# Expert stage of a two-layer trunk: PSUM banks of the gather, scatter and one-hot steps taken in turn from two pools

## The chip, the cores and the metric

The kernel runs on one core of a Trainium2 chip. The metric is the device time of one execution in microseconds (us). Most executions of one kernel agree within 0.3%. The engines are named as the profile names them: PE (TensorE, matmuls; PEld are its weight loads), DVE (VectorE), ACT (ScalarE), POOL (GpSimd) and SP (SyncE, which issues the transfers).

## The reference

A post-norm trunk of two layers on 256 tokens of width 1024. Each layer has a mixing sublayer (three groups of heads) and a channel sublayer: a dense SwiGLU in layer 0, and in layer 1 eight SwiGLU experts of inner width 3584, of which each token uses two:

```python
logits = (xt @ w_router).astype(jnp.float32)
top_v, top_i = lax.top_k(logits, TOP_K)                 # TOP_K = 2 of N_EXPERTS = 8
top_w = jax.nn.softmax(top_v, axis=-1)
gates = jnp.sum(jax.nn.one_hot(top_i, N_EXPERTS) * top_w[..., None], axis=1)
for e in range(N_EXPERTS):
    y = y + gates[:, e:e+1] * ((jax.nn.silu(xt @ w_gate[e]) * (xt @ w_up[e])) @ w_down[e])
x = layer_norm(DN_ALPHA * x + y, ln2_g[l], ln2_b[l])
```

## The kernel before

All weights are float32 and come from memory once. A weight chunk of 128x2048 (`raw`) is split into a rounded high part on ACT (`whi`, line 151) and the rest on DVE (`wlo`, line 152), and a product of such numbers is three matmuls: high by high, low by high, high by low (`mm3`, lines 161 to 163). For the expert stage only the tokens that chose an expert are used. Experts are handled in pairs (pr = e // 2).

The expert stage is `moe`. It goes over 8 experts e and 7 pieces m of the inner width (512 each). I call one pair (e, m) a pass. A pass has three blocks of matmuls: gate (G, tile `eg`), up (U, tile `eg`), and the down product of the pass before (D, tiles `y`, two banks that are held for all 7 passes of an expert). Each block needs two split chunks, one for each half of the block, so that a pass has six splits on ACT and six on DVE. Between G and U stands the transpose of the pass before (`ht`, line 166), which is copied out by ACT and DVE (`wk`, lines 943 and 945).

An expert with at most 64 tokens takes a light form at run time (lines 897, 898 and 971: two matmuls instead of three); otherwise the heavy form runs (lines 161 to 163). Both stand in the program, behind a branch (line 856) that reads a register. In this run experts 0, 3, 5 and 6 are heavy, and 1, 2, 4 and 7 light.

Between the blocks the kernel does small steps, one at each `point()`. A list `chores` holds them, and three points lie in each pass (behind G, behind U, behind D):

- gather (`gx`, line 741): one-hot matrices `pm` pick the tokens of the next pair of experts. Eight steps, one for each quarter of the width, high part (`xth`) and low part (`xtl`); four matmuls each. A high step is copied out by ACT (line 751, two copies), a low step by DVE (line 749, two copies). This happens in passes m = 2 to 4 of experts 1, 3 and 5.
- one-hot step (`gsb`, lines 800 and 802): the transposed one-hot matrix and the gate weights of one expert, copied out by ACT (lines 805, 806). Two steps in each of experts 0, 2, 4 and 6.
- scatter (`sc`, lines 993 and 994): adds an expert's result to the tokens. Four steps in passes m = 1 and 2 of the expert that follows, each added to `r` (the residual) by one DVE instruction (line 999).

PSUM is used through two pools of four tiles of 128x512 float32 each: `acc` and `wps`. In the expert stage `wps` holds the `eg` tiles, two for each pass, and `acc` holds the two `y` tiles and, in the two banks that are left, `ht` and the steps:

```python
acc = ctx.enter_context(tc.tile_pool(name="acc", bufs=4, space=PS))
wps = ctx.enter_context(tc.tile_pool(name="wps", bufs=4, space=PS))
def bank(pool, name):
    return pool.tile([P, 512], F32, tag="acc" if pool is acc else "wps", name=name)
```

The copies out of PSUM are held back by `defer(n, ...)` until n more half-splits (1024 wide) are recorded. The framework's scheduler gives each tile a bank when one is free, and puts every engine's instructions in an order by that; an instruction that writes a bank waits for the last reader of the tile that had it before. So which bank a step gets decides both the order on the engines and the waits. Blocks behind a branch stay whole.

Of the kernel before, what the change touches and what calls it, by code (L numbers as in the profile page):

```python
# [86 lines left out]
def trunk(ctx: ExitStack, tc: tile.TileContext, x, consts, mconsts, vecs, lnrows, w_in, w_uq, w_ukv, w_o,  # L87
# [6 lines left out]
# [5 lines that stand above are left out]
# [38 lines left out]
    last = [None, None]  # L137
# [17 lines left out]
    def hold_splits(*steps):  # L155
        plan.clear()
        for ins, eng, n in steps:
            plan.extend([(ins, eng)] * n)
# [18 lines left out]
    def ln_sum(r, src, ps, s, scale=ALPHA, halves=(0, 1)):  # L177
        for n in halves:
            cs = slice(n * 512, (n + 1) * 512)
            nc.vector.scalar_tensor_tensor(r[:, cs], src[:, cs], scale, ps[n], ALU.mult, ALU.add, accum_out=s[:, n:n + 1])  # L180
            ln_half(r, n, s)
# [455 lines left out]
    def moe(pool, raws2, raws3, r, gb, rw):  # L637
# [87 lines left out]
        def gather(pr):  # L725
            pm = pool.tile([P, 2, 256], F32R, tag="pm", name="pm")
            for tt in range(2):
                for j in range(2):
                    ip = nc.vector.tensor_scalar(pm[:, tt, j * P:(j + 1) * P], iota, posm[:, tt, 2 * pr + j:2 * pr + j + 1],
                                            None, ALU.is_equal)  # L730
            if pr == 0:
                hold_splits(((), None, 2), ((pw,), nc.gpsimd, 2), ((i1, pw), nc.gpsimd, 1), ((i1, ip), None, 3))
            xgs = [pool.tile([P, KD, P, 2], F32R, tag="xg", name="xg", bufs=3) for j in range(2)]

            def half_part(k2, hl, n=0):
                src = (xth, xtl)[hl]
                b = bank(acc, "gx")
                for kk in range(2):
                    k = 2 * k2 + kk
                    for tt in range(2):  # L740
                        nc.tensor.matmul(b[:, kk * 256:(kk + 1) * 256], src[:, tt, k * P:(k + 1) * P], pm[:, tt, :],
                                         start=(kk == 0 and tt == 0), stop=(kk == 1 and tt == 1))

                def copies():
                    bv = b.rearrange("p (a b) -> p a b", b=256)
                    for j in range(2):
                        o = xgs[j][:, 2 * k2:2 * k2 + 2, :, hl]
                        if hl:
                            nc.vector.tensor_copy(o, bv[:, :, j * P:(j + 1) * P])
                        else:  # L750
                            nc.scalar.copy(o, bv[:, :, j * P:(j + 1) * P])

                defer(n, copies)

            def part(k2):
                for hl in range(2):
                    half_part(k2, hl)

            return pm, xgs, part, half_part
# [26 lines left out]
        def gather2(pr, pm):  # L786
            gs = pool.tile([P, 2], F32, tag="gs", name="gs")
            pT = pool.tile([P, 2, 2, P], F32R, tag="pTm", name="pTm")
            sc[pr] = [(gs[:, j:j + 1], pT[:, j]) for j in range(2)]

            for j in range(2):
                for tt in range(2):
                    nc.vector.tensor_scalar(pm[:, tt, j * P + 64:(j + 1) * P], iota[:, 64:P],
                                            posds[0][:, tt, 2 * pr + j:2 * pr + j + 1], None, ALU.is_equal)
            pmf = pm.bitcast(F32)

            def one(j):
                b = bank(acc, "gsb")
                for tt in range(2):
                    nc.tensor.matmul(b[:, 256:264], pmf[:, tt, j * P:(j + 1) * P], gates[:, tt, :], start=(tt == 0), stop=False)  # L800
                for tt in range(2):
                    nc.tensor.matmul(b[:, tt * P:(tt + 1) * P], pmf[:, tt, j * P:(j + 1) * P], ident, start=False, stop=(tt == 1))

                def copies():
                    nc.scalar.copy(gs[:, j:j + 1], b[:, 256 + 2 * pr + j:257 + 2 * pr + j])
                    nc.scalar.copy(pT[:, j, :, :], b[:, 0:256].rearrange("p (a b) -> p a b", b=P))

                defer(CHORE_N, copies)

            return one  # L810
# [3 lines left out]
        def defer(n, fn):  # L814
            if n:
                later.append([n, fn])
            else:
                fn()


        chores = []
        points = [0]

        def point():
            points[0] += 1
            if chores and chores[0][0] <= points[0]:
                chores.pop(0)[1]()
# [161 lines left out]
            nc.vector.scalar_tensor_tensor(y[1], yb[n], gs, y[0].bitcast(F32), ALU.mult, ALU.subtract)  # L989

        def scatter(n, tt, y, pT, last=False):
            b = bank(acc, "sc")
            nc.tensor.matmul(b, pT[:, tt, :], y[0], start=True, stop=False)
            nc.tensor.matmul(b, pT[:, tt, :], y[1], start=False, stop=True)
            if last:
                ln_sum(ya[tt], ya[tt], {n: b}, fsums[tt], 1.0, (n,))
            else:
                cs = slice(n * 512, (n + 1) * 512)
                defer(CHORE_N, lambda: nc.vector.tensor_tensor(ya[tt][:, cs], ya[tt][:, cs], b, ALU.add))
# [80 lines left out]
        sc = {}  # L1080
# [5 lines left out]
        def finish(e, m, ht, fold_up=None, fe=None, hook=None):  # L1086
            if m == 0:
                yb[e] = [bank(acc, "y") for _ in range(2)]
            down(e, m, ht, yb[e], fold_up, fe, hook)
            if m == FM - 1:  # L1090
                gs, pT = sc[e // 2][e % 2]
                if e == NE - 1:
                    ys = [[wk[:, 1024 * n + 512 * i:1024 * n + 512 * i + 512] for i in range(2)] for n in range(2)]
                    for n in range(2):
                        scaled(n, yb[e], gs, ys[n])
                    for n in range(2):
                        for tt in range(2):
                            scatter(n, tt, ys[n], pT, True)
                else:
                    yt = pool.tile([P, 2, 2, 512], F32R, tag="xg", name="ys", bufs=3)  # L1100
                    ys = [[yt[:, n, i] for i in range(2)] for n in range(2)]

                    def both():
                        for n in range(2):
                            scaled(n, yb[e], gs, ys[n])

                    defer(4, both)
                    for n in range(2):
                        for tt in range(2):
                            chores.append((points[0] + 3, lambda n=n, tt=tt: scatter(n, tt, ys[n], pT)))  # L1110
# [19 lines left out]
        for e in range(NE):  # L1130
            pr = e // 2
# [163 lines left out]
    with tc.tile_pool(name="spl2", bufs=3, reuse_waits="tile") as spl[0], \  # L1295
            tc.tile_pool(name="moe", bufs=1, reuse_waits="tile") as mp, tc.tile_pool(name="raws3", bufs=ORDER.count(2), reuse_waits="tile") as raws3, \
            tc.tile_pool(name="raws2", bufs=ORDER.count(1), reuse_waits="tile") as raws2:
        xo = moe(mp, raws2, raws3, r, gb, rw)
        for tt in range(2):
            for n in range(2):  # L1300
                cs = slice(n * 512, (n + 1) * 512)
                nc.sync.dma_start(out[0, tt * P:(tt + 1) * P, cs], xo[tt][:, cs])
# [108 lines left out]
```

## Time and profile before

| what | value |
|---|---|
| median of 3 runs | 1471.09 us (1469.09 to 1473.74) |
| the profiled execution | 1468.16 us, span 1466.0 us |
| PE busy | 1359.3 us, 93% of the span |
| DVE busy | 1176.5 us, 80% |
| ACT busy | 997.0 us, 68% |
| mean granted TensorE clock | 0.987 of full speed |

The expert stage runs from about 485 us to 1450 us. Busy shares are means over passes of two kinds, so the table of stretches in the rows below is read pass by pass: a heavy pass without steps takes 17.1 us and a light one 14.4 us. A stretch there goes from one `ht` to the next, so it holds U and D of one pass and G of the next. Its columns are: from:to and the length in us, then the busy time (and instructions) of PE, PEld, DVE, ACT and POOL, the granted TensorE clock (1.00 is full speed), the share of time in which the 16 DMA engines were busy, and GB/s. The profiled execution lies 2.93 us under the median of the runs.

### The profile page before, as it was taken

The numbers are of one execution on the slowest core, as the hardware profiler recorded it, in microseconds if no ns is written. First come the engines' busy times: TensorE is split into PE (matmuls) and PEld (weight loads), VectorE is DVE, ScalarE is ACT, GpSimd is POOL, SyncE is SP. The second block draws the span as 40 slices with busy tenths as digits, with TensorE's granted clock in tenths as the row PEclk, the third lists the DMA queues.
The fourth block names the chain that finished last, engine by engine and source line by source line (L and its number), as shares of the span: only waits on it lengthen the run. The fifth ranks groups of instructions, "written<-read, shape, count | busy, mean of one in ns | idle before, by whom it ended". The sixth has DMA issues, their size and how long they took to land. (4 is left out here: it accounts for less than half of the span.)

```text
span 1466.0 us, 18597 instructions
## 1 busy us (share of the span) xinstructions
PE 1359.3 (93%) x6927; PEld 1118.0 (76%) x6927; DVE 1176.5 (80%) x1256; ACT 997.0 (68%) x1073; POOL 78.4 (5%) x113
## 2 busy tenths in 40 slices
PE   7999999999999899988989999998999999999895
PEld 6987999998987688766666677866677787787663
DVE  6577655557677788899999987898998788788996
ACT  3564444444565677788978877787986777778794
POOL 3011000004102100000000000000000000000101
PEclk9999999999999999999999999999999999999998
DMA  6733555544534699999999998899998799899980
GB/s 264 276 135 115 189 186 186 188 157 153 194 116 201 231 339 356 375 365 349 420 406 369 419 382 323 325 367 348 407 419 342 295 357 357 311 358 389 357 363 30
DMA packets 63513, 429.46 MB, mean 293 GB/s; under 512 B 7058, under 2 KB 7570, under 8 KB 15268
## 3 DMA queue, kind: packets, MB, share of 16 engines
q1 hardware_dynamic: 63364, 427.81, 76.4%
q8 instruction: 81, 1.33, 0.4%
q14 instruction: 36, 0.29, 0.1%
q0 software_dynamic: 32, 0.03, 0.0%
HBM read 426.76 MB, written 1.05 MB: 292 GB/s over the span
## 5 line engine op out<-in xcount | busy, mean ns | idle before, releaser
L152 DVE TENSOR_TENSOR wlo<-raw,whi 128x2048 fp32r<-128x2048 f32 (+4 forms) x475 | 911.0, 1939 | 158.3 <-ACT whi L151 156.7
L151 ACT CAST whi<-raw 128x2048 fp32r<-128x2048 f32 (+4 forms) x482 | 771.0, 1619 | 250.5 <-PE gu L585 44.0
L898 PE MATMUL eg<-wlo,xg 128*128 128x512 f32 x448 | 185.6, 414 | 22.1 <-DVE wlo L152 19.0
L162 PE MATMUL eg<-wlo,xg 128*128 128x512 f32 x448 | 178.0, 397 | 0.8 <-DVE wlo L152 0.3
L161 PE MATMUL eg<-whi,xg 128*128 128x512 f32 x448 | 178.6, 399 | 0.0
L897 PE MATMUL eg<-whi,xg 128*128 128x512 f32 x448 | 178.4, 398 | 0.0
L163 PE MATMUL eg<-whi,xg 128*128 128x512 f32 x448 | 176.6, 394 | 0.0
L898 PEld LDWEIGHTS eg<-wlo,xg 128*128 128x128 f32 x448 | 84.4, 188 | 70.4 <-DVE wlo L152 54.9
L971 PE MATMUL y<-wlo,wk 128*128 128x512 f32 x224 | 94.2, 421 | 17.0 <-DVE wlo L152 15.8
L162 PEld LDWEIGHTS eg<-wlo,xg 128*128 128x128 f32 x448 | 86.9, 194 | 21.5 <-DVE wlo L152 5.4
L163 PEld LDWEIGHTS eg<-whi,xg 128*128 128x128 f32 x448 | 86.7, 194 | 17.3
L584 PE MATMUL gu<-xhi,whi 128*128 128x256 f32 x352 | 99.8, 283 | 0.1
L585 PE MATMUL gu<-xlo,whi 128*128 128x256 f32 x352 | 99.7, 283 | 0.2 <-DVE xlo L224 0.2
L161 PEld LDWEIGHTS eg<-whi,xg 128*128 128x128 f32 x448 | 86.9, 194 | 16.7
L586 PE MATMUL gu<-xhi,wlo 128*128 128x256 f32 x352 | 99.6, 283 | 0.0
L897 PEld LDWEIGHTS eg<-whi,xg 128*128 128x128 f32 x448 | 84.9, 189 | 15.0 <-ACT whi L151 0.5
L971 PE MATMUL y<-whi,wk 128*128 128x512 f32 x224 | 90.3, 403 | 3.6 <-DVE wk L945 1.5
L162 PE MATMUL y<-wlo,wk 128*128 128x512 f32 x224 | 88.0, 393 | 3.6 <-DVE wlo L152 3.4
L161 PE MATMUL y<-whi,wk 128*128 128x512 f32 x224 | 87.5, 392 | 0.4 <-ACT hh L919 0.4
L163 PE MATMUL y<-whi,wk 128*128 128x512 f32 x224 | 87.3, 390 | 0.0
L971 PEld LDWEIGHTS y<-wlo,wk 128*128 128x128 f32 x224 | 44.1, 197 | 42.7 <-DVE wlo L152 36.0
L584 PEld LDWEIGHTS gu<-xhi,whi 128*128 128x128 f32 x352 | 67.6, 192 | 0.7 <-DVE xlo L224 0.3
(313 smaller groups left out, 2111.8 us busy)
## 6 DMA issues: line engine op xcount, KB each, us to landing
raw<-in_e_gate SPq DMA_DIRECT2D x112, 1024.0 KB, 7.1
raw<-in_e_up SPq DMA_DIRECT2D x110, 1024.0 KB, 7.2
raw<-in_e_down SPq DMA_DIRECT2D x108, 1024.0 KB, 7.4
raw<-in_ffn_gu SPq DMA_DIRECT2D x22, 1024.0 KB, 4.8
raw<-in_ffn_dn SPq DMA_DIRECT2D x11, 1024.0 KB, 4.7
raw<-in_w_in SPq DMA_DIRECT2D x10, 960.0 KB, 4.7
raw<-in_w_o SPq DMA_DIRECT2D x8, 1024.0 KB, 6.7
gb<-in_lnrows SPq DMA_DIRECT2D x8, 512.0 KB, 5.3
```

The lines of the kernel that those rows point to most:

```text
L151: last[0] = nc.scalar.copy(hi[:, :n], src)
L152: last[1] = (eng or nc.vector).tensor_tensor(lo[:, :n], src, hi.bitcast(F32)[:, :n], ALU.subtract)
L161: nc.tensor.matmul(o, ahi, bhi, start=start, stop=False)
L162: nc.tensor.matmul(o, ahi, blo, start=False, stop=False)
L163: return nc.tensor.matmul(o, alo, bhi, start=False, stop=stop)
L584: nc.tensor.matmul(o, hi[:, cs], xhi[:, k, :], start=(g == 0 and k == 0), stop=False)
L585: nc.tensor.matmul(o, hi[:, cs], xlo[:, k, :], start=False, stop=False)
L586: nc.tensor.matmul(o, lo[:, cs], xhi[:, k, :], start=False, stop=(g == 1 and k == 7))
L897: nc.tensor.matmul(bs[g], x2, sp[k // 4][0][:, cs], start=(k == 0), stop=False)
L898: nc.tensor.matmul(bs[g], x2, sp[k // 4][1][:, cs], start=False, stop=(k == 7))
L971: nc.tensor.matmul(yb[n], h2, sp[j // 2][i][:, j % 2 * D + n * 512:j % 2 * D + n * 512 + 512], start=(m == 0 and j == 0 and i == 0), stop= ...
```

## The change

A counter gives the steps their pool: odd ones take a bank of `wps`, even ones one of `acc`. The first pair's gather, before the stage begins, and the last expert's scatter keep `acc`. Nothing else is changed: the same instructions run on every engine, and SP's and POOL's orders stay as they were.

```diff
@@ half_part (gather) @@
-                b = bank(acc, "gx")
+                b = bank(acc, "gx") if pr == 0 else step_bank("gx")
@@ one (one-hot step) @@
-                b = bank(acc, "gsb")
+                b = step_bank("gsb")
@@ before point() @@
+        turns = [0]
+
+        def step_bank(name):
+            turns[0] += 1
+            return bank((acc, wps)[turns[0] % 2], name)
@@ scatter @@
-            b = bank(acc, "sc")
+            b = bank(acc, "sc") if last else step_bank("sc")
```

Line numbers behind `point()` are 5 higher in the changed kernel (743 to 797 are the same in both). By the count, scatter steps 1 and 3, all high gather steps and the first one-hot step take `wps`; scatter steps 2 and 4, all low gather steps and the second one-hot step take `acc`.

Since banks come free at other moments, the order changes. On PE in expert 3, from the transposes of pass 3 to the gather steps of pass 4, before (a gather step is one row of four matmuls; L856 is the branch ahead of U or D):

```order
L166 MATMUL ht_9207<-mc_70,hh_8945 128x128 x4
L741 MATMUL gx_9272<-pm_9131,xth_4902 128x256 x4
L741 MATMUL gx_9336<-pm_9131,xtl_4903 128x256 x4
L741 MATMUL gx_9409<-pm_9131,xth_4902 128x256 x4
L856 COMPARE_AND_BRANCH
...
L166 MATMUL ht_9414<-mc_70,hh_9143 128x128 x4
L741 MATMUL gx_9479<-pm_9131,xtl_4903 128x256 x4
L741 MATMUL gx_9543<-pm_9131,xth_4902 128x256 x4
L856 COMPARE_AND_BRANCH
...
L741 MATMUL gx_9607<-pm_9131,xtl_4903 128x256 x4
```

The same place in the changed kernel:

```order
L166 MATMUL ht_9207<-mc_70,hh_8945 128x128 x4
L741 MATMUL gx_9336<-pm_9131,xtl_4903 128x256 x4
L861 COMPARE_AND_BRANCH
...
L741 MATMUL gx_9272<-pm_9131,xth_4902 128x256 x4
L861 COMPARE_AND_BRANCH
...
L741 MATMUL gx_9409<-pm_9131,xth_4902 128x256 x4
L166 MATMUL ht_9414<-mc_70,hh_9143 128x128 x4
L741 MATMUL gx_9479<-pm_9131,xtl_4903 128x256 x4
L741 MATMUL gx_9607<-pm_9131,xtl_4903 128x256 x4
L861 COMPARE_AND_BRANCH
...
L741 MATMUL gx_9543<-pm_9131,xth_4902 128x256 x4
```

Before, three steps stood between G and U of pass 3, and all three shared one bank (gx_9272, gx_9336, gx_9409); now one stands there, one behind U, and one ahead of the next `ht`. In pass 4 two steps in one bank still follow each other: gx_9479 and gx_9543 before, gx_9479 and gx_9607 now.

On DVE, from the copies of that pass 4 to the split of D's second half (`wlo` are splits, L749 copies of low gather steps, L945 the transposes' copy, L793 writes the one-hot matrix anew), before:

```order
L152 TENSOR_TENSOR wlo_9424<-raw_9419,whi_9423 128x2048
L749 CAST xg_9136<-gx_9479 128x256
L749 CAST xg_9137<-gx_9479 128x256
L152 TENSOR_TENSOR wlo_9428<-raw_9421,whi_9427 128x2048
L945 TENSOR_TENSOR wk_5038<-ht_9414,wk_5038 128x4x128
L152 TENSOR_TENSOR wlo_9489<-raw_9484,whi_9488 128x2048
L749 CAST xg_9136<-gx_9607 128x256
L749 CAST xg_9137<-gx_9607 128x256
L793 TENSOR_SCALAR pm_9131<-mc_70,gt_5207 128x64 x4
L152 TENSOR_TENSOR wlo_9493<-raw_9486,whi_9492 128x2048
```

And now:

```order
L152 TENSOR_TENSOR wlo_9424<-raw_9419,whi_9423 128x2048
L749 CAST xg_9136<-gx_9479 128x256
L749 CAST xg_9137<-gx_9479 128x256
L749 CAST xg_9136<-gx_9607 128x256
L749 CAST xg_9137<-gx_9607 128x256
L152 TENSOR_TENSOR wlo_9428<-raw_9421,whi_9427 128x2048
L950 TENSOR_TENSOR wk_5038<-ht_9414,wk_5038 128x4x128
L152 TENSOR_TENSOR wlo_9489<-raw_9484,whi_9488 128x2048
L793 TENSOR_SCALAR pm_9131<-mc_70,gt_5207 128x64 x4
L152 TENSOR_TENSOR wlo_9493<-raw_9486,whi_9492 128x2048
```

Two copies went from behind D's first split (wlo_9489) to ahead of U's second split (wlo_9428).

On DVE in passes 1 and 2 of the same expert (L999 before, L1004 now, adds a scatter step), before:

```order
L999 TENSOR_TENSOR r_4872<-r_4872,sc_8942 128x512
L999 TENSOR_TENSOR r_4863<-r_4863,sc_9003 128x512
L152 TENSOR_TENSOR wlo_8957<-raw_8950,whi_8956 128x2048
...
L152 TENSOR_TENSOR wlo_9016<-raw_9011,whi_9015 128x2048
L999 TENSOR_TENSOR r_4872<-r_4872,sc_9070 128x512
L152 TENSOR_TENSOR wlo_9020<-raw_9013,whi_9019 128x2048
```

And now:

```order
L1004 TENSOR_TENSOR r_4872<-r_4872,sc_8942 128x512
L152 TENSOR_TENSOR wlo_8957<-raw_8950,whi_8956 128x2048
...
L152 TENSOR_TENSOR wlo_9016<-raw_9011,whi_9015 128x2048
L1004 TENSOR_TENSOR r_4863<-r_4863,sc_9003 128x512
L1004 TENSOR_TENSOR r_4872<-r_4872,sc_9070 128x512
L749 CAST xg_9136<-gx_9202 128x256
L152 TENSOR_TENSOR wlo_9020<-raw_9013,whi_9019 128x2048
```

One add left the place ahead of G's second split (wlo_8957); that add and one gather copy now stand ahead of U's second split (wlo_9020).

## Rows read from the trace of the kernel before

**Rows 1.** Page, part 1: busy us, share of the span, instructions, by engine.

```profile
PE 1359.3 (93%) x6927; PEld 1118.0 (76%) x6927; DVE 1176.5 (80%) x1256; ACT 997.0 (68%) x1073; POOL 78.4 (5%) x113
```

**Rows 2.** Stretches: a plain heavy pass, expert 3's passes 2 to 4; then light, expert 1.

```profile
933.60:950.70 17.10, 17.10 (x78) 14.18 (x77) 14.86 (x8) 13.39 (x10) 0.00 (x0) 1.00 0.95 359
...
872.20:892.10 19.90, 19.04 (x87) 15.32 (x86) 16.00 (x12) 12.06 (x12) 0.00 (x0) 1.00 0.86 320
892.10:912.80 20.70, 19.01 (x90) 15.71 (x89) 15.53 (x10) 16.32 (x15) 0.00 (x0) 1.00 0.84 315
912.80:933.60 20.80, 19.12 (x90) 15.64 (x88) 16.65 (x16) 13.96 (x12) 0.00 (x0) 1.00 0.79 299
696.40:710.80 14.40, 13.48 (x55) 9.49 (x54) 14.40 (x9) 12.97 (x10) 0.00 (x0) 1.00 1.01 419
...
645.60:661.70 16.10, 14.27 (x65) 10.93 (x64) 15.83 (x12) 11.87 (x11) 0.00 (x0) 1.00 0.96 365
661.70:679.50 17.80, 15.00 (x67) 11.12 (x66) 15.44 (x11) 15.96 (x15) 0.00 (x0) 1.00 0.96 356
679.50:696.40 16.90, 14.28 (x67) 11.15 (x66) 16.55 (x17) 13.68 (x12) 0.00 (x0) 1.00 0.96 343
```

**Rows 3.** Waits of PE, 480 to 1466 us: total us, times, longest us.

```profile
PE gx L741 <- DVE xg L749: 5.6, 6, 0.9
...
PE gsb L800 <- DVE r L999: 2.3, 3, 0.8
PE gx L741 <- DVE r L999: 2.3, 3, 0.8
PE gx L741 <- ACT xg L751: 2.2, 3, 0.8
```

**Rows 4.** Timeline, expert 3 pass 3: start us, us, engine, line, form, [idle before].

```profile
892.46 0.71 PE L741 MATMUL gx<-pm,xth 128*128 128x256 f32 x4
893.21 0.66 ACT L751 CAST xg<-gx 128x256 fp32r<-128x256 f32 x2 [4.60 <-PE gx L741]
...
893.93 0.73 PE L741 MATMUL gx<-pm,xtl 128*128 128x256 f32 x4 [0.75 <-ACT xg L751]
894.70 0.76 DVE L749 CAST xg<-gx 128x256 fp32r<-128x256 f32 x2 [3.25 <-PE gx L741]
...
895.60 0.71 PE L741 MATMUL gx<-pm,xth 128*128 128x256 f32 x4 [0.94 <-DVE xg L749]
895.70 2.29 DVE L152 TENSOR_TENSOR wlo<-raw,whi 128x2048 fp32r<-128x2048 f32 x1 [0.24 <-ACT whi L151]
...
896.15 0.40 PE L161 MATMUL eg<-whi,xg 128*128 128x512 f32 x1
```

**Rows 5.** Timeline, expert 3 pass 2, PE and DVE, from scatter step 4 on.

```profile
872.86 0.39 PE L994 MATMUL sc<-ys,pTm 128*128 128x512 f32 x1
873.28 0.69 DVE L999 TENSOR_TENSOR r<-r,sc 128x512 f32<-128x512 f32 x1 [1.01 <-PE sc L994]
...
874.02 0.75 PE L741 MATMUL gx<-pm,xth 128*128 128x256 f32 x4 [0.78 <-DVE r L999]
```

**Rows 6.** Timeline, expert 3 pass 4: DVE ahead of D's second half, and PE there.

```profile
921.62 0.76 DVE L749 CAST xg<-gx 128x256 fp32r<-128x256 f32 x2 [1.97 <-PE gx L741]
922.29 0.74 DVE L793 TENSOR_SCALAR pm<-mc,gt 128x64 fp32r<-128x64 f32 x4
922.94 4.49 DVE L152 TENSOR_TENSOR wlo<-raw,whi 128x2048 fp32r<-128x2048 f32 x2
...
924.16 0.39 PE L161 MATMUL y<-whi,wk 128*128 128x512 f32 x1
925.28 0.50 PE L162 MATMUL y<-wlo,wk 128*128 128x512 f32 x1 [0.74 <-DVE wlo L152]
```

**Rows 7.** Timeline, expert 1 (light) pass 3, DVE.

```profile
664.33 0.76 DVE L749 CAST xg<-gx 128x256 fp32r<-128x256 f32 x2 [1.60 <-PE gx L741]
...
665.32 2.29 DVE L152 TENSOR_TENSOR wlo<-raw,whi 128x2048 fp32r<-128x2048 f32 x1 [0.23 <-ACT whi L151]
```

## The prediction

> **What bounds the kernel now.** I read the page's busy shares first: PE is busy for 1359.3 of 1466.0 us [rows 1], so an idle stretch of PE is worth looking for. A mean hides two kinds of pass, so the table of stretches came next [rows 2]. A heavy pass without steps takes 17.10 us and PE is busy for all of it: there PE is the bound, and DVE (14.86) has 2.2 us to spare. A light pass without steps takes 14.40 us and DVE is busy for all of it: there DVE is the bound and PE (13.48) waits. So a wait of PE costs time in heavy passes, a wait of DVE in light ones, and nothing else does. The steps that the change touches fall on heavy experts 3, 5 (scatter, gather) and 6 (scatter, one-hot), on light experts 1 (scatter, gather), 2, 4 (scatter, one-hot) and 7 (scatter), and on expert 0 (one-hot).
>
> In the heavy gather, passes 2 to 4 take 19.90, 20.70 and 20.80 us [rows 2]. The list of waits then says whom PE waits for at steps [rows 3]: six times for a low gather copy on DVE (5.6 us), three times for the ACT copy of a high step (2.2), three times for a scatter add ahead of a gather step (2.3), three times for the same ahead of a one-hot step (2.3). With three gathers (experts 1, 3, 5) that is four waits a gather, all for a bank of `acc`. The timeline shows one [rows 4]: a gather step ends at 893.17, its two ACT copies at 893.87, the next step starts at 893.93 because it writes the same bank; it ends at 894.66, its DVE copies run from 894.70 to 895.46, the third step starts at 895.60.
>
> **The change part by part.** No instruction is added or taken away, so the sum holds only waits that go, stay or come. I worked out in the built program, for each step and block, which tile had its bank before and where the last reader of that tile stands on its engine. Before, the four waits of a gather are those above. In the changed program two of the four are left in each gather: the low step that follows scatter step 4 takes that step's bank (gx_9202), and of the two low steps that follow each other in pass 4 the second takes the first one's (gx_9607). The high steps, in `wps`, take banks whose readers stand ahead of splits that PE has already used. The same holds for every G, U and D block: the last reader of its bank stands ahead of a split that the block needs anyway, so the `eg` tiles get no new wait.
>
> A wait costs more than its idle time, since the matmuls behind it start anew. From start to start a gather step takes 0.55 us when nothing holds it (895.60 to 896.15); the two that waited took 1.47 and 1.67 [rows 4], so an ACT wait costs 0.92 and a DVE wait 1.12.
>
> Pass 3, heavy: both waits go, 2.04 us. The stretch agrees: 20.70 less 17.10 less three steps of 0.55 is 1.95. What comes late next is U's second split. It stands behind the copies of the one low step that is left between `ht` and U. A step that starts at t ends at t + 0.71, its copies at t + 1.5, the split (2.29) at t + 3.7. U starts at t + 0.55, and its second half needs the low part after 13 matmuls of about 0.23 (half of 24 in 17.10 us for 72, one on), at t + 3.6. So some 0.15 us come back, and the gain is 1.9.
>
> Pass 4, heavy: the DVE wait of 1.12 stays. The second wait of that pass goes: D's second half waits 0.74 for a split that stands behind two copies (0.76) and four one-hot instructions (0.74) [rows 6]; start to start it is 1.12 instead of 0.23, so it costs 0.89. Afterwards only the four one-hot instructions stand there; they wait for the last gather step, now a high one behind U, which ends when the low one did, and the copies' 0.67 is off the queue. I keep 0.1 of it. The two copies now stand ahead of U's second split, which by the sum of pass 3 costs 0.15. Gain 0.65.
>
> Pass 2, heavy: 19.90 less 17.10, less two gather steps (1.1) and one scatter step (0.5) leaves 1.2. The wait for the add of scatter step 4 is 1.16 from start to start (872.86 to 874.02) [rows 5] where 0.23 is free: 0.93. It stays, and stands behind one more add, which runs while the transposes and step 4 do. The other 0.3 is D's second split, late because a pair of low copies stands ahead of it; one of the pair has moved up, and the second scatter step's add no longer shares its place ahead of G's second split with the third's. I count 0.4 for both.
>
> Heavy gather: 1.9 + 0.65 + 0.4 = 2.95, two of them (experts 3 and 5): 5.9.
>
> Light gather (expert 1): DVE's idle time counts. The three stretches hold 0.27, 2.36 and 0.35 us [rows 2], 2.98 in all; most is 1.60 for the second step of pass 3, which had itself waited for the ACT copies, and 0.23 for an ACT split behind them [rows 7]. Afterwards pass 3 has one low step right behind `ht`, which DVE reaches as it ends: 0.1. But pass 2 gets a new wait: the low step waits for the add of step 4, and its first copy stands next on DVE, so DVE idles through a step, 0.71 and its start: 0.85. In pass 4 the two pairs of low copies each wait, 0.45 and 0.8. That is 2.2, a gain of 0.8.
>
> Scatter and one-hot steps in the other experts: their waits for an add stay (the first one-hot step still takes scatter step 4's bank), and the ACT copies of both one-hot steps still stand together. Bounds: 0.3 either way for each of five; I take 0.
>
> Sum: 5.9 + 0.8 = 6.7. Against the profiled execution, 1468.16 - 6.7 = 1461.5; the median lies 2.93 higher, so the forecast is 1471.09 - 6.7 = **1464.4 us**.
>
> [...]
>
> **The rivals.** (1) All bank waits go in effect. A wait that is left could fall into time that PE or DVE spends otherwise. The two that are left cost 0.93 and 1.12 in each heavy gather, 4.1 in two; expert 6's one-hot wait is worth 0.9 and the light gather's rest 1: 6.7 + 6 gives 1458. For it: DVE has 4 us idle in the heavy passes. Against it: that idle time is itself the wait for PE's steps. (2) The waits only move. PE gains at the steps and gives it back at the next split, because splits come just in time; each of the six heavy passes would return some 1 us, 5.9 in all, and the light gather 0.8: 1471. For it: in pass 3 my own sum has U's second split 0.1 late. Against it: DVE's spare 2.2 us in a heavy pass. (3) Slower: `wps` lacks a bank. A high step or scatter step holds one of its four banks while G or U wants two, and the block waits for copies that stand behind a split on ACT. The price is 1.12 a wait, as for a low step; there are 15 steps in `wps` in experts 3, 5 and 6 (four high and two scatter steps in each gather expert, two scatter steps and a one-hot step in expert 6). From six or seven of them on the change loses; all of them would make 16.8 - 6.7 = 10 us, 1481. Against it: the bank readers that I traced all stand early enough.
>
> [...]
>
> **How the numbers follow.** Forecast 0.65 (its own range 1461.5 to 1468, from gains of 3 to 9.5: only pass 3's waits in heavy passes at the one end; at the other 0.3 more at each of five scatter places and the late splits at nothing), rival 1 0.07, rival 2 0.2, rival 3 0.08. The range that leaves 2 in 10 out reaches from 1459.5 to 1471. About 0.3% (4.4 us) is what a measurement of this kernel can tell from no change: faster than 1466.7 takes nine tenths of the forecast, all of rival 1 and a little of rival 2, 0.68; slower than 1475.5 is most of rival 3, 0.07; the rest is 0.25.
>
> **What would show it right or wrong.** In the profile after, PE's waits for ACT at gather steps are gone, those for DVE copies fall from six to three, and those for adds stay at three. The heavy gather's stretches read about 19.5, 18.8 and 20.1 us, plain passes still 17.1 and 14.4. In expert 1 pass 3 falls to about 15.5, while pass 2 grows. I am wrong if PE shows waits at `eg` or `y` for ACT copies (rival 3), if waits for `wlo` at `eg` and `y` in heavy passes grow by as much as those at `gx` fall (rival 2), or if plain passes change.

## The result and the profile after

The changed kernel is slower: 1491.36 us (median of 4 runs, 1489.54 to 1494.35) against 1470.09 us for the kernel before in the same comparison (1466.88 to 1473.74). The ratio is 1.0143, with a 95% interval of 1.0118 to 1.0167. The forecast was 1464.4 us, and the time lies 20 us above the range.

The page of the changed kernel, part 1 (busy us, share of the span, instructions); the span is 1489.0 us where it was 1466.0:

```profile
PE 1374.1 (92%) x6927; PEld 1128.0 (76%) x6927; DVE 1177.6 (79%) x1256; ACT 995.6 (67%) x1073; POOL 78.8 (5%) x113
```

DVE and ACT work as long as before. PE reads 15 us busier with the same matmuls [rows 1], which hints at matmuls that ran longer. The stretches of the gather passes (columns as in [rows 2]), expert 3's passes 2 to 4 and then expert 1's:

```profile
883.10:906.44 23.34, 20.73 (x87) 16.48 (x86) 16.82 (x12) 13.78 (x12) 0.00 (x0) 0.93 0.78 285
906.50:927.51 21.01, 19.17 (x90) 15.41 (x89) 15.34 (x10) 11.91 (x11) 0.00 (x0) 1.00 0.79 287
927.50:951.27 23.77, 20.99 (x91) 16.64 (x90) 16.93 (x16) 16.15 (x15) 0.00 (x0) 0.93 0.74 276
647.70:667.15 19.45, 15.26 (x65) 10.80 (x64) 16.12 (x13) 13.68 (x12) 0.00 (x0) 1.00 0.89 329
667.20:686.47 19.27, 16.06 (x68) 12.28 (x67) 16.31 (x11) 11.81 (x11) 0.00 (x0) 0.91 0.95 348
686.40:706.82 20.42, 16.24 (x68) 12.38 (x67) 16.12 (x17) 15.70 (x15) 0.00 (x0) 0.92 0.80 297
```

The heavy passes take 3.4, 0.3 and 3.0 us more than in [rows 2], the light ones 3.3, 1.5 and 3.5 us more. Expert 5's passes 2 to 4 take 23.33, 21.00 and 22.23 us. Plain passes still take 17.07 and 14.40 us, and the scatter and one-hot passes of the other experts are within 0.5 us of before. So the loss, about 20 us, lies in the nine gather passes. (The stage starts 2.3 us later than before, too, but that isn't the change: over all the profiled kernels here its start lies between 508 and 514 us, behind code that none of them changes. So I compare passes.)

The waits of PE in the expert stage (total us, times, longest us) and those of ACT, in the changed kernel:

```profile
PE y L162 <- DVE wlo L152: 12.9, 8, 1.8
...
PE gx L741 <- DVE xg L749: 2.8, 3, 0.9
...
PE gsb L800 <- DVE r L1004: 2.3, 3, 0.8
PE gx L741 <- DVE r L1004: 2.3, 3, 0.8
```

```profile
ACT xg L751 <- PE gx L741: 47.0, 12, 5.2
```

The same line of ACT, and that of PE at `y`, in the kernel before:

```profile
ACT xg L751 <- PE gx L741: 12.4, 3, 4.6
...
PE y L162 <- DVE wlo L152: 3.4, 4, 1.7
```

At the steps PE does what was predicted: no wait for ACT copies, three instead of six for DVE copies, three each for adds [rows 3]. But ACT now waits for all twelve high gather steps, 47 us, and PE waits 12.9 us at `y` in heavy D blocks, where it was 3.4 us. The timeline of expert 3's pass 2 shows the link (start us, us, engine, line, operation, [idle before]):

```profile
884.73 1.92 ACT L151 CAST whi<-raw 128x2048 fp32r<-128x2048 f32 x1
...
884.98 0.74 PE L741 MATMUL gx<-pm,xtl 128*128 128x256 f32 x4 [0.78 <-DVE r L1004]
...
885.56 0.40 PE L161 MATMUL eg<-whi,xg 128*128 128x512 f32 x1
...
891.15 0.63 PE L741 MATMUL gx<-pm,xth 128*128 128x256 f32 x4
...
891.82 0.66 ACT L751 CAST xg<-gx 128x256 fp32r<-128x256 f32 x2 [5.18 <-PE gx L741]
...
892.36 1.91 ACT L151 CAST whi<-raw 128x2048 fp32r<-128x2048 f32 x1
...
894.30 2.29 DVE L152 TENSOR_TENSOR wlo<-raw,whi 128x2048 fp32r<-128x2048 f32 x1 [2.79 <-ACT whi L151]
...
896.65 0.50 PE L162 MATMUL y<-wlo,wk 128*128 128x512 f32 x1 [1.83 <-DVE wlo L152]
```

ACT makes D's first split until 886.65 and then comes to the two copies of the high step. That step now stands behind U on PE and ends at 891.78, so ACT waits 5.18 us. D's second split comes behind the copies on ACT, DVE's part of it from 894.30, and PE, which began D at 891.62, runs out of work after 13 matmuls. Pass 3 has the same chain, and so has the light pass 3:

```profile
913.93 0.66 ACT L751 CAST xg<-gx 128x256 fp32r<-128x256 f32 x2 [3.94 <-PE gx L741]
...
918.76 0.50 PE L162 MATMUL y<-wlo,wk 128*128 128x512 f32 x1 [1.83 <-DVE wlo L152]
...
673.91 0.67 ACT L751 CAST xg<-gx 128x256 fp32r<-128x256 f32 x2 [3.23 <-PE gx L741]
...
678.74 0.52 PE L976 MATMUL y<-wlo,wk 128*128 128x512 f32 x1 [1.81 <-DVE wlo L152]
```

In pass 2, ACT's order at this place is the one before, split, two copies, split; only PE moved the step (ACT's queue in both kernels, then PE before and PE after):

```
ACT   whi_9077 | xg<-gx_9138 x2 | whi_9081
PE    before   ht_9006  sc_9070  gx_9138  [U]  gx_9202  [D]
PE    after    ht_9006  sc_9070  gx_9202  [U]  gx_9138  [D]
```

Behind the wait there is a second loss. A table of three short stretches of pass 2: 12 matmuls of D ahead of the wait, and two stretches behind it (from:to, length, busy PE, PEld, DVE, ACT, POOL, granted clock, DMA, GB/s):

```profile
892.09:894.36 2.27, 2.27 (x12) 1.73 (x10) 0.06 (x1) 2.27 (x4) 0.00 (x0) 1.00 1.01 350
896.99:899.90 2.91, 2.91 (x10) 2.26 (x9) 2.83 (x2) 1.95 (x2) 0.00 (x0) 0.61 0.68 236
898.00:900.90 2.90, 2.90 (x8) 2.22 (x8) 2.90 (x2) 1.09 (x1) 0.00 (x0) 0.50 0.89 353
```

After an idle time of 1.83 us the granted clock falls to 0.50, until about the end of D: matmuls start every 0.23 us ahead of the wait, and every 0.43 us from 898.14 to 900.27. This happens in pass 2 of experts 3 and 5 and in pass 4 of expert 3 (0.93 over the pass), not in pass 3 (1.00, behind a wait of 1.83 us in both experts), and not in expert 5's pass 4 (22.23 us, 1.00), whose code and wait (1.82 us) are those of expert 3's. In expert 1's passes 3 and 4 the clock is lower, too (0.91 and 0.92 over the pass); no run parts its share there from that of the wait.

### The profile page after: what moved, and what is told of

Its sections match the earlier page's. It is cut to its first block, busy times and chain, and to the rows that moved or that the text cites. A ratio compares the mean times of both kernels' runs of the same rounds, so it can differ in the third digit from the quotient of the medians.

```text
span 1489.0 us, 18598 instructions
## 1 busy us (share of the span) xinstructions
PE 1374.1 (92%) x6927; PEld 1128.0 (76%) x6927; DVE 1177.6 (79%) x1256; ACT 995.6 (67%) x1073; POOL 78.8 (5%) x113
## 5 line engine op out<-in xcount | busy, mean ns | idle before, releaser
L152 DVE TENSOR_TENSOR wlo<-raw,whi 128x2048 fp32r<-128x2048 f32 (+4 forms) x475 | 910.7, 1938 | 181.6 <-ACT whi L151 180.2
L162 PE MATMUL eg<-wlo,xg 128*128 128x512 f32 x448 | 178.5, 398 | 0.7 <-DVE wlo L152 0.3
L976 PE MATMUL y<-wlo,wk 128*128 128x512 f32 x224 | 97.3, 434 | 20.2 <-DVE wlo L152 19.3
L162 PEld LDWEIGHTS eg<-wlo,xg 128*128 128x128 f32 x448 | 87.1, 194 | 23.1 <-DVE wlo L152 6.7
L162 PE MATMUL y<-wlo,wk 128*128 128x512 f32 x224 | 90.4, 404 | 12.9 <-DVE wlo L152 12.9
L976 PE MATMUL y<-whi,wk 128*128 128x512 f32 x224 | 92.7, 414 | 4.9 <-ACT whi L151 2.2
L161 PE MATMUL y<-whi,wk 128*128 128x512 f32 x224 | 89.9, 403 | 0.3 <-ACT hh L924 0.3
L163 PE MATMUL y<-whi,wk 128*128 128x512 f32 x224 | 89.3, 398 | 0.0
L585 PEld LDWEIGHTS gu<-xlo,whi 128*128 128x128 f32 x352 | 68.3, 194 | 0.6 <-DVE xlo L224 0.4
```

What stands on the lines that cost most here:

```text
L152: last[1] = (eng or nc.vector).tensor_tensor(lo[:, :n], src, hi.bitcast(F32)[:, :n], ALU.subtract)
L161: nc.tensor.matmul(o, ahi, bhi, start=start, stop=False)
L162: nc.tensor.matmul(o, ahi, blo, start=False, stop=False)
L163: return nc.tensor.matmul(o, alo, bhi, start=False, stop=stop)
L585: nc.tensor.matmul(o, hi[:, cs], xlo[:, k, :], start=False, stop=False)
L976: nc.tensor.matmul(yb[n], h2, sp[j // 2][i][:, j % 2 * D + n * 512:j % 2 * D + n * 512 + 512], start=(m == 0 and j == 0 and i == 0), stop= ...
```

## The experiments

Two theories. The ACT-queue theory is the chain above. The bank theory is the prediction's third rival: steps hold banks of `wps` that G and U want.

| run | what it is | median us (low to high) | ratio to before in the same comparison, 95% interval |
|---|---|---|---|
| e1 | only gather alternates | 1495.43 (1494.14 to 1497.63) | 1.0166 (1.0143 to 1.0189) |
| e2 | only scatter and one-hot alternate | 1471.30 (1469.64 to 1473.96) | 1.0001 (0.9990 to 1.0012) |
| e3 | changed kernel, high copies held | 1475.63 (1470.87 to 1478.77) | 1.0028 (1.0013 to 1.0043) |
| e4 | before, low steps in `wps` | 1473.79 (1470.98 to 1477.16) | 1.0019 (1.0004 to 1.0034) |
| e5 | e3, one-hot matrix held too | 1463.95 (1462.39 to 1464.66) | 0.9954 (0.9938 to 0.9970) |
| e6 | changed kernel, PE busy in the wait | 1487.55 (1485.06 to 1488.65) | 1.0113 (1.0090 to 1.0135) |
| e7 | e5, all copies held | 1453.95 (1450.65 to 1455.15) | 0.9883 (0.9859 to 0.9906) |
| e8 | before, with the holds of e7 | 1455.84 (1454.80 to 1456.73) | 0.9900 (0.9880 to 0.9921) |
| e9 | e7, scatter adds held too | 1442.82 (1441.10 to 1444.69) | 0.9797 (0.9775 to 0.9820) |
| e10 | before, with the holds of e9 | 1447.61 (1443.65 to 1450.04) | 0.9838 (0.9820 to 0.9857) |
| e11 | e9 once more, beside e10 | 1443.21 (1440.75 to 1445.65) | 0.9812 (0.9795 to 0.9830) |

**e1 and e2: which part of the change.** e1 undoes two of the three edits, e2 the third.

```diff
 e1   b = bank(acc, "gsb")                                        # one-hot, scatter as before
 e2   b = bank(acc, "gx")                                         # gather as before
```

> Only the gather steps of experts 2 to 7 alternate between the two groups; one-hot and scatter steps stay in acc, as before. On PE each high gather step stands behind U, as in the changed kernel, and its two copies on ACT ahead of D's second split. ACT-queue theory (ACT waits for a high step that PE runs only behind U, so D's second split is late and PE waits in D): the loss lies in the gather passes alone, so nearly all of it stays: 1489 us, between 1485 and 1493, ACT idle ahead of the high copies 40 us or more. Bank theory (steps hold banks of wps that G and U want; six scatter and one-hot steps fewer hold one here): the loss shrinks by the share of those steps, to about 1483.

> Only the one-hot and scatter steps alternate; all gather steps stay in acc, where each high one stands ahead of U. ACT-queue theory: no high copy waits behind U, so within 2 us of the kernel before, 1468 to 1472. Bank theory: a third of the steps in wps is left, and so about a third of the loss: 1477.

The gather alone makes the whole loss, and the scatter and one-hot steps alone make none: e1 is no faster than the changed kernel, though all scatter and one-hot steps are out of `wps`. (It is 4 us slower by the medians, with intervals of the two ratios that overlap; by its passes 1.6 us are expert 5's pass 4, where the clock fell this time.) It also lies 2.4 us above the ACT-queue theory's range. For the bank theory both times are wrong; that its expectations counted too few scatter steps in `wps` (there are more of them than of high gather steps) makes that plainer.

**e3: the same order on PE, ACT's copies later.**

```diff
-                            nc.scalar.copy(o, bv[:, :, j * P:(j + 1) * P])
+                            with after(*last[:1] if n else ()):   # behind the last split recorded
+                                nc.scalar.copy(o, bv[:, :, j * P:(j + 1) * P])
```

> The changed kernel with one thing more: the ACT copies of a high gather step are issued behind the split of raw that was issued last when they come up, which puts them behind D's second split instead of ahead of it. PE's order is that of the changed kernel, and the steps hold their banks in wps longer. ACT-queue theory: ACT's idle time at the high copies falls from 47 us to under 10, D's second split is on time, the gather passes of the heavy experts read about 19.3, 18.9 and 19.5 us, and the whole takes about 1464 us, between 1458 and 1472. Bank theory: held longer, the banks cost as much or more: 1491 or above.

ACT's wait at the high copies falls from 47.0 to 2.3 us:

```profile
ACT xg L752 <- PE gx L741: 2.3, 3, 1.0
```

Of the 21 us of loss 4.4 are left (1475.63 against 1471.20 us for the kernel before in the same comparison). That is 3.6 us above the expected range. The heavy passes 2 and 3 read 19.56 and 18.80 us, as expected; pass 4 does not: 24.41 in expert 3, 22.80 in expert 5. Its timeline in expert 3 (L794 rewrites the one-hot matrix, L152 are splits, L162 at `y` is D):

```profile
926.79 0.63 PE L741 MATMUL gx<-pm,xth 128*128 128x256 f32 x4
...
927.34 0.58 DVE L794 TENSOR_SCALAR pm<-mc,gt 128x64 fp32r<-128x64 f32 x3 [2.69 <-PE gx L741]
...
927.83 2.28 DVE L152 TENSOR_TENSOR wlo<-raw,whi 128x2048 fp32r<-128x2048 f32 x1
...
930.17 0.50 PE L162 MATMUL y<-wlo,wk 128*128 128x512 f32 x1 [2.52 <-DVE wlo L152]
```

The hold moved DVE's order: three of the four rewrites stand ahead of D's first split, and wait there for the last high step, again one behind U. It is the same mechanism on the other engine, made by my experiment.

**e4: as many gather steps in `wps`, but low ones.**

```diff
-                b = bank(acc, "gx")
+                b = bank(acc, "gx") if pr == 0 or hl == 0 else bank(wps, "gx")
```

> The kernel before with the low gather steps in wps and the high ones in acc: as many gather steps in wps as in the changed kernel, but now low ones, whose copies are DVE's. PE then runs the high steps ahead of U and low ones behind it. ACT-queue theory: ACT's idle time at high copies is as before (about 12 us) and the time near the kernel before: 1470, between 1464 and 1475. Bank theory: as many steps in wps as in the changed kernel, so as slow: 1485 or above.

Four steps of each gather hold a bank of `wps` here, as many as in the changed kernel, and the median is 2.6 us above the kernel before (1473.79 against 1471.20), not the 15 or more that the bank theory asks for: it falls. That the time came out near its forecast is in part luck, for the forecast of ACT's wait was a miss. The wait doubled, and PE's waits for U's second split in heavy passes grew from 0.3 to 5.1 us. Against that, the six waits of PE at `gx` for low copies (5.6 us before) are gone:

```profile
ACT xg L751 <- PE gx L741: 26.3, 6, 5.1
...
PE eg L162 <- DVE wlo L152: 5.1, 7, 1.8
```

Expert 3's pass 4 shows where the new wait comes from. The high step stands ahead of U here, and its copies ahead of U's second split:

```profile
920.09 0.66 ACT L751 CAST xg<-gx 128x256 fp32r<-128x256 f32 x2 [4.61 <-PE gx L741]
...
920.63 1.91 ACT L151 CAST whi<-raw 128x2048 fp32r<-128x2048 f32 x1
...
922.57 2.29 DVE L152 TENSOR_TENSOR wlo<-raw,whi 128x2048 fp32r<-128x2048 f32 x1 [4.28 <-ACT whi L151]
...
924.92 0.51 PE L162 MATMUL eg<-wlo,xg 128*128 128x512 f32 x1 [1.82 <-DVE wlo L152]
```

It is the chain of the changed kernel at another block. The length of ACT's idle time doesn't tell its price: 4.60 us ahead of U's second split cost PE nothing in the kernel before [rows 4], where two more steps stood ahead of U, and 4.61 us cost 1.82 here. What sets the two apart is whether the split behind it is late for its block.

**e5: e3 without its new wait.** The four rewrites become a chore of their own at the end of the gather, held behind a split.

```diff
+            chores.append((0, lambda: second_half(pr, half[pr][0])))   # the four rewrites
 ...
+        def second_half(pr, pm):
+            with after(*dve if pr else ()):
 ...
```

> The kernel of e3 with one thing more: the four instructions on DVE that rewrite the second half of the one-hot matrix (they may run only when the last gather step has read it) are issued at the end of the gather, behind a subtraction of the pass after, instead of where they come ready, which in e3 was ahead of D's first subtraction of pass 4. ACT-queue theory (one in-order queue that holds an instruction for a step behind U ahead of a split of D is the whole loss): in e3 pass 4 lost to the same mechanism on DVE. So passes 2 and 3 stay at e3's 19.6 and 18.8 us, pass 4 falls from 24.4 and 22.8 to about 19.6 (heavy) and from 20.1 to about 17 (light), and the whole is about 11 us below e3: 1464 us, between 1460 and 1469. Bank theory (pass 4 is slow because its steps hold banks of wps or wait in one bank): pass 4 stays above 22 us and the whole at 1475.

Expert 3's passes 2 to 4, and PE's wait at `y` in heavy passes:

```profile
873.30:892.85 19.55, 18.77 (x88) 15.38 (x87) 16.72 (x12) 13.84 (x12) 0.00 (x0) 1.00 0.86 328
892.80:911.60 18.80, 18.79 (x89) 15.53 (x88) 15.34 (x10) 13.98 (x13) 0.00 (x0) 1.00 0.90 343
911.60:931.60 20.00, 19.05 (x90) 15.61 (x89) 16.10 (x12) 14.36 (x14) 0.00 (x0) 1.00 0.80 301
...
PE y L162 <- DVE wlo L152: 1.9, 2, 1.7
```

Expected were 19.6, 18.8 and 19.6. The wait at `y`, 12.9 us in the changed kernel, is 1.9. With PE's order as in the changed kernel, and only copies and rewrites moved on ACT and DVE, the loss of 21 us has become a gain of 6. That the gain is the banks' is not shown: no run gives the kernel before the holds of e5 alone, and e8 below shows that holds pay there, too.

**e6: the clock by itself.**

```diff
+                    if j == 2 and e in (3, 5) and m in (1, 2, 3):
+                        for _ in range(8):
+                            nc.tensor.matmul(yb[0][0:64], fo[:, :, 1], sp[0][0][:, 0:512], start=False, stop=False)
```

> The changed kernel with eight more matmuls of 512 columns in each D of the three gather passes of the heavy experts 3 and 5, between its two halves, where PE waits 1.83 us for the late split. They multiply by zeros and add nothing to the result; eight at 0.23 us take 1.84 us, the time of the wait. Clock theory (beside the wait, passes 2 and 4 lose 1.5 us because PE's granted clock reads 0.50 for some 3 us after the wait): with PE busy through the wait the clock stays at 1.00, so pass 2 of experts 3 and 5 and pass 4 of expert 3 fall from 23.3 and 23.8 to about 21.8 and 22.2 us, and pass 3, whose clock did not fall, stays at 21.0; in all 4 us less, 1487. If the slow matmuls behind the wait have another cause (late data), they stay slow, and the time is that of the changed kernel, 1491, or up to 2 us more a pass.

```profile
884.90:906.70 21.80, 20.95 (x96) 16.38 (x95) 16.72 (x12) 13.82 (x12) 0.00 (x0) 1.00 0.77 289
906.70:927.72 21.02, 20.92 (x98) 16.52 (x97) 15.34 (x10) 11.92 (x11) 0.00 (x0) 1.00 0.82 304
927.70:949.89 22.19, 21.16 (x98) 16.52 (x97) 16.84 (x16) 16.17 (x15) 0.00 (x0) 1.00 0.73 271
```

The clock stays at 1.00. The three passes in which it had fallen get shorter by 1.54, 1.56 and 1.58 us, and the three in which it had not stay within 0.02. The matmuls behind the wait were slow by the clock, then, and not by late data. So of what a heavy pass loses, about 1.55 us are the clock, where it falls; the late split is about 2.2 (e6's passes less e5's).

**e7 to e11: how far the holds go, and what the banks are worth.** e7 holds the low copies and the copies of the one-hot steps as well, e9 the scatter adds too; e8 and e10 are the kernel before with the same holds.

```diff
 e7   with after(*dve if n else ()):  nc.vector.tensor_copy(o, ...)          # low copies
 e7   with after(last[0]):            nc.scalar.copy(gs..., ...); nc.scalar.copy(pT..., ...)
 e9   with after(dve[0]):             nc.vector.tensor_tensor(ya[tt][:, cs], ya[tt][:, cs], b, ALU.add)
```

> The kernel of e5, and also the low copies on DVE and the four ACT copies behind the one-hot steps are issued behind the split that was issued last when they come up. No copy of a step stands ahead of a split that the current block still needs. ACT-queue theory: the heavy gather's passes read about 19.2, 18.5 and 18.8 us, expert 6's one-hot pass falls from 22.4 to about 20, those of experts 2 and 4 from 19.6 to about 17, and the whole takes about 1454 us, between 1447 and 1463. Bank theory: no better than e5.

> The kernel before (all steps in acc) with the same holds as e7. It tells what the holds are worth without the alternating banks, and e7 less e8 is what the banks are worth once no queue waits. ACT-queue theory: the holds help here too (ACT waited 26 us for gather and one-hot steps before, DVE 20), but steps that share a bank wait for copies that now come later: about 1460 us, between 1452 and 1470, and e7 is 3 to 10 us faster. Bank theory: e8 is the faster one.

> The kernel of e7, and also the scatter adds on DVE are issued behind the subtraction that was issued last when they come up. If a copy or add that stands ahead of a split costs time wherever it waits for PE, the scatter passes fall too (pass 1 of experts 3, 5 and 6 from 19.3 us to about 18.5, of the light ones from 17.95 to about 17.3): 6 us less than e7, 1448, between 1443 and 1453. Against it: DVE waits only 9 to 11 us for scatter steps in all, and an add that comes later holds its bank longer, which the next scatter or gather step may want: then 1454 or above.

> The kernel before (all steps in acc) with the holds of e9: beside e11 it tells what the alternating banks are worth when no copy or add stands ahead of a split. In e8 the banks of acc cost PE a wait of 0.5 us for the ACT copies of six gather steps, and e7 was 2 us below e8. With the adds later too, a scatter step waits for the add of the one before it in the same bank: about 1449 us, between 1444 and 1455, 3 to 8 us above e11. If the banks are worth nothing any more: the same as e11.

> The kernel of e9 once more, beside e10 on the same chip: 1443 us, between 1440 and 1446, and below e10 by 3 to 8 us if the alternating banks still save waits, by nothing if they don't.

The times of e7, e8, e10 and e11 lie where they were expected. e9 lies 0.2 us below its range: pass 2 of experts 3, 5 and 6 fell by 1.0 us each as well, which the expectation hadn't counted. And e7 is only 1.9 us below e8, not 3 to 10. In e8 the waits at gather steps for ACT copies are the expected ones:

```profile
PE gx L741 <- ACT xg L753: 2.9, 6, 0.6
```

In e11, expert 3's passes 1 to 4:

```profile
847.80:866.58 18.78, 18.77 (x83) 15.31 (x82) 17.14 (x12) 13.44 (x11) 0.00 (x0) 1.00 1.01 414
866.60:885.12 18.52, 18.52 (x87) 15.49 (x86) 15.62 (x10) 13.80 (x12) 0.00 (x0) 1.00 0.92 332
885.10:903.68 18.58, 18.58 (x89) 15.67 (x88) 16.53 (x13) 13.99 (x13) 0.00 (x0) 1.00 0.95 353
903.70:922.24 18.54, 18.54 (x90) 15.61 (x89) 15.13 (x10) 14.37 (x14) 0.00 (x0) 1.00 0.91 331
```

PE is busy for all of passes 2 to 4, and a pass costs its plain 17.1 us and its steps. This version is 28 us faster than the kernel before (1443.21 against 1471.02). The holds do nearly all of it. What the alternating banks add is small and only roughly known: e11's median is 4.4 us below e10's and e7's 1.9 below e8's, but in both pairs the intervals of the ratios overlap; by the passes of the profiles it is 2.2 and 2.3 us.

## Why the prediction was wrong

**Terms that held.** At PE's steps every wait went or stayed as the sum had it. With the new wait out of the way (e5), the heavy gather gains 0.35, 1.90 and 0.80 us in passes 2, 3 and 4 against [rows 2]; predicted were 0.4, 1.9 and 0.65. This agreement doesn't prove the sizes, for e5 also holds copies and rewrites that the kernel before doesn't: e8, with more holds and no alternating banks, reads 19.54, 19.14 and 19.35 us in the same passes, so holds without the banks can give pass 2's gain, most of pass 3's and more than pass 4's. The scatter and one-hot steps at zero held in e2. That two waits of four would stay in each gather held, too. The light gather's 0.8 came out at 0.4 in e5: passes 2 to 4 give 1.1 and the moved rewrites cost 0.65 in pass 5.

**The step that failed** is the sentence that "a wait of PE costs time in heavy passes, a wait of DVE in light ones, and nothing else does", which put every new wait of ACT at nothing, and with it the paragraphs on passes 2 to 4. They follow each moved step along PE and its copies along DVE. They say that a high step now stands behind U ("now a high one behind U, which ends when the low one did"), and ask there only what DVE's rewrites wait for. Where the copies of that high step stand on ACT was not asked: ahead of D's second split, in pass 2 at the very place they had before. A low step behind U, as before, holds DVE alone, and cost PE 0.74 us in pass 4 [rows 6]; a high step behind U holds ACT, and through ACT DVE as well, since each split passes from the one to the other (5.18 us and 2.79 us idle in expert 3's pass 2). That is 2.2 us in each of six heavy passes (from e6's 21.80, 21.02 and 22.19 to e5's 19.55, 18.80 and 20.00), 13.3 in all; 1.55 for the clock in three of them, 4.7; and 9.4 less 0.65 in expert 1 (19.45, 19.27, 20.42 to 16.77, 16.05, 16.91), wait and clock together. Together 26.7 us, and from the changed kernel to e5 the medians fall by 27.4.

The row for it was there. [rows 4] shows ACT idle for 4.60 us for a high step that PE ran late. The prediction reads that row for PE's waits and their price, and does not ask what the late copies hold up behind them on ACT. In that row the copies stand ahead of U's second split, and U stood behind two more steps anyway, so the wait did no harm there. The claim that `eg` tiles get no new wait was right and did not help: it looks at banks.

**The rivals.** The third had the right side, slower, with a loss of 10 us where 21 were measured, but by a mechanism that e1, e2 and e4 rule out; the sign that it named, waits at `eg` or `y` for the ACT copies of steps, does not show. What showed was in the second rival's list: waits for `wlo` at `y` in heavy passes grew by 9.5 us, more than those at `gx` fell (5.0). It assumed that splits come just in time and would only give back what was won. No rival had the clock.

## What to carry to other kernels

A buffer given to a step moves the step in its engine's order; follow then every queue that holds an instruction waiting for that step (here ACT's, idle for 5.18 us in pass 2), up to the next instruction that the critical engine needs behind it. A copy out of PSUM that nobody needs soon belongs behind the split that is needed next: such holds of copies, adds and rewrites were worth 23 us here without any new bank (e10), and the banks some 2 more by the passes. An idle gap of the matmul engine cost nearly twice its length where the clock fell behind it: 1.83 us idle and 1.55 for the clock.

## What the hardware showed beyond expectation

The granted clock fell to 0.50 after a single idle time of PE of 1.83 us in some passes and not in others with the same code and the same idle time (in pass 4, behind 1.82 us, it fell in expert 3 and not in expert 5; in e1 it fell in both). Expert 1's pass 2 took 19.45 us at 1.00 in the changed kernel and 20.08 us at 0.92 in e6, which leaves that pass alone. No run here shows what decides whether it falls. Eight matmuls by zeros in the gap kept it at 1.00 in all six heavy gather passes (e6), and passes where it hadn't fallen took the same time within 0.02 us.
